# Other byte offsets for the operands of the split-fp32 matmuls in a four-layer encoder trunk

## Chip, cores and metric

One core of a Trainium2 chip runs the whole program. The metric is the time of one execution on the device, in microseconds (us).

## What is computed

The reference is a trunk of four layers for 256 tokens of width 1024: RWKV-7 time mixing in layers 0 and 3, stick-breaking attention in layer 1, sparse attention over selected keys in layer 2. Each layer is followed by a SwiGLU block of inner width 2816, and every sub-layer has an RMS norm ahead and a residual add behind:

```
for i in range(DEPTH):
    h = rms_norm(x, norm_mix[i])
    ...
    x = x + y
    x = x + swiglu(rms_norm(x, norm_ffn[i]), ffn_w_gu[i], ffn_w_down[i])

def swiglu(h, w_gu, w_down):
    g, u = jnp.split(h @ w_gu, 2, axis=-1)
    return (jax.nn.silu(g) * u) @ w_down
```

All of it is in float32.

## The kernel before, in words

Activations lie transposed: 128 features on the partitions, 256 tokens along them. Weights come from memory in pieces of 128 x 1024 float32 values (512 KB), each by one DMA on the queue of SyncE into one of four tiles `raw`.

Most products are made not as plain fp32 matmuls but of three fp32r matmuls. `piece` (line 905) rounds a weight piece to `wh` (a copy to fp32r on ScalarE or VectorE) and takes the rest `wl = raw - wh` (VectorE, line 913). Activations are split in the same way, into a high half and a low half that lie behind each other. Then `x*w` is `xh*wh + xl*wh + xh*wl`. The weight tiles are the stationary operand, loaded into the array by LDWEIGHTS, 128 columns (512 bytes of a partition) at a time, and the activations are the moving operand, read as a stream of 256 or 512 columns. There are five slots of 4096 bytes in a partition for `wh` and four for `wl`, counted out by the planner; one of the tiles `wh0` to `wh3` and `wl0` to `wl4` names each of them.

Three shapes of such products matter here.

- A *pair* (`gemm1`, line 955, and the down projection in `ffn`): a stream of 512 columns, `xh` and `xl` behind each other, against `wh`, then one of 256 columns, `xh`, against `wl`. The tiles `gate`, `up`, `dn` and `qk` are made of pairs. While the stream of 512 runs, the following `wl` is loaded; while that of 256 runs, the next `wh`.
- A *triple* (`mm3`, in `gemm2`, line 966, and `out_half`, line 979): three streams of 256 columns, against `wh`, `wh` again and `wl`. These are `kp`, `rp` and `po`, and `pg`.
- A *turned* triple (`v_gemm`, line 1626, and its like): the weights are the moving operand, 512 columns of `wh`, `wl` and `wh`, and the activations `xg` are loaded. These are `vps`, `k`, `q` and `qi`.

The moving activations lie in four large slots of 16 KB: `xb` (`xg`, for pairs and turned triples), `SA`, `SZ` and `PR` (`h` of the SwiGLU blocks; `prx` of `rp` is in `SZ`, `kx` of `kp` in `PR`). The activations of `po` (`yhl`, `ohl`) lie in two other slots, `s0` and `s1`.

The order of all instructions is planned beforehand: `Plan.schedule` simulates the engines with a table of costs, and `Plan.emit` writes the instructions out in that order. The costs take no account of where a tile lies. `emit` first allocates the tiles of SBUF in the order of the list `LAYOUT` (line 65), one behind the other, each rounded up to 32 bytes. A name such as `SA_0` is a slot. So a tile's address follows from what stands ahead of it in `LAYOUT`. In the version before, the constant `eps_rms` (4 bytes, hence 32) stands ahead of `xb_0 SZ_0 PR_0 SA_0`.

In the addresses of the built program that gives these remainders by 128 bytes:

| tiles | before |
|---|---|
| `wh`, `wl`, `raw` | 0, 0, 0 |
| `xb`, `SZ`, `PR`, `SA` | 32 |
| `s0`, `s1` (`yhl`, `ohl`) | 0 |
| `s6`, `s7` (`gus` and others), `xt` | 0 |

Of the kernel before, what the change touches and what calls it, by code (L numbers as in the profile page):

```python
# [14 lines left out]
F32R = mybir.dt.float32r  # L15
# [18 lines left out]
PIECE = 1024  # L34
# [22 lines left out]
for _n, _w in CONSTS:  # L57
# [6 lines left out]

LAYOUT = (
    "ones xt0 chmask xt1 xt2 xt3 sqa_0 QC_0 sq_0 s0_0 raw_0 s1_0 t_0 s6_0 raw_1 raw_2 t_1 t_2 t_3 raw_3 wh_0 wl_0 "
    "wh_1 wh_2 wh_3 t2_0 xm_0 t2_1 xm_1 xm_2 consts0 wl_1 xm_3 identb t2_2 wl_2 t_4 t2_3 wl_3 s7_0 t2_4 dc_0 vf0 vf1 "
    "vf3 vf2 t_5 t_6 t_7 kc0_0 kc1_0 kc2_0 eps_rms xb_0 SZ_0 PR_0 SA_0 lim eps_gn vecs omka kks_0").split()


class Region:
# [759 lines left out]
def trunk(ctx: ExitStack, tc: tile.TileContext, xT_in, vecs_in, wts, lora_in, consts_in, id32_in, nqk_in, outT, order, layers=None):  # L831
# [11 lines left out]
    def T(shape, group=None, name="t", dtype=F32):  # L843
        return plan.tile(sb, [P] + list(shape), dtype, group, name)
# [41 lines left out]
    identb = T([P], name="identb", dtype=BF16)  # L886
    eps_rms, eps_gn = T([1], name="eps_rms"), T([1], name="eps_gn")
    anye.memset(eps_rms, 1e-6)
    lim = T([2], name="lim")
# [3 lines left out]
    omka = T([2, NC], name="omka")  # L893
# [7 lines left out]
    def f(ap):  # L901
        return ap.bitcast(F32)


    def piece(key):

        i = len(order)
        order.append(key)
        r = T([PIECE], "raw", f"raw{i}")
        sp.dma_start(r, wts[i])  # L910
        h, l = T([PIECE], "wh", f"wh{i}", F32R), T([PIECE], "wl", f"wl{i}", F32R)
        anye.copy(h, r)
        dve.tensor_tensor(l, r, f(h), op=ALU.subtract)
        return h, l
# [40 lines left out]
    def gemm1(key, x, name, group="g"):  # L955


        out = bank(name, group)
        wh, wl = [v3(t, NC) for t in piece(key)]
        for c in range(NC):  # L960
            with unit():
                pe.matmul(out, wh[:, c], flat(x[:, c]), start=(c == 0), stop=False)
                pe.matmul(out[:, :S], wl[:, c], x[:, c, 0], start=False, stop=(c == NC - 1))
        return out

    def gemm2(key, xs, name):

        out = bank(name, "g")
        for c in range(NC):
            if c % 4 == 0:  # L970
                wh, wl = [v3(t, 4) for t in piece(key + (c // 4,))]
            with unit():
                for i in range(2):
                    sl = slice(i * P, (i + 1) * P)
                    mm3(out[:, i * S:(i + 1) * S], (wh[:, c % 4, sl], wl[:, c % 4, sl]), xs(c),
                        start=(c == 0 and i == 0), stop=(c == NC - 1 and i == 1))
        return out

    def out_half(key, half, xs, after):

        for j in range(4):
            o = bank("po", "g")
            wh, wl = [v3(t, 4) for t in piece(key + (half, j))]
            for k in range(4):
                with unit():
                    for n in range(2):
                        sl = slice(n * P, (n + 1) * P)
                        mm3(o[:, n * S:(n + 1) * S], (wh[:, k, sl], wl[:, k, sl]), xs(k),
                            start=(k == 0 and n == 0), stop=(k == 3 and n == 1))
            dve.tensor_tensor(xt[j], xt[j], ab(o), op=ALU.add)  # L990
            if half == 1:
                after(j)
# [1108 lines left out]
```

## Time and profile before

| | |
|---|---|
| median of 3 runs | 1358.36 us (1357.81 to 1359.17) |
| the profiled execution | 1358.13 us |
| its span in the profile | 1356.1 us |
| TensorE clock granted, mean | 0.999 |
| instructions | 26070 |

A profile is one execution, taken by the hardware profiler. PE is TensorE's matmuls and PEld its weight loads, DVE is VectorE, ACT ScalarE, POOL GpSimd and SP SyncE, whose queue issues the DMAs. Nearly every instruction carries line 827, where `emit` writes it out, so groups are told apart by the names of their tiles. The recorded duration of a matmul reaches from its start to an end that is modelled, and the next one starts before that: the spacing of the starts is what TensorE takes. Some records of matmuls can be missing.

### The profile page before, as it was taken

What the parts mean: (1) busy time and instruction counts of PE and PEld (TensorE: products, weight loads), DVE (VectorE), ACT (ScalarE), POOL (GpSimd) and SP (SyncE); (2) the same over time, 40 slices, a digit from 0 to 9 for tenths busy, and PEclk for the clock granted to TensorE, in tenths of its full rate; (3) what the DMA queues carried; (4) which work ended last, traced back from release to release, by engine and by line L of the source; (5) the groups of instructions that cost most, each with busy time, mean ns of one, the idle gap of its engine ahead of it and who ended that gap; (6) DMA issues with size and microseconds to landing.
All of it is one profiled execution on the core that took longest, in us unless ns stands there. A gap on an engine that the chain in (4) does not pass through costs nothing.

```text
span 1356.1 us, 26070 instructions
## 1 busy us (share of the span) xinstructions
PE 1335.6 (98%) x10480; PEld 1168.0 (86%) x10480; DVE 1119.4 (83%) x1932; ACT 777.9 (57%) x1301; POOL 8.8 (1%) x22
## 2 busy tenths in 40 slices
PE   8999899999999999999999999999999999999998
PEld 7997798888888898888887798888899877988887
DVE  8998789886676779886679988888589997988864
ACT  7945665545466755544456876555378366655442
POOL 0000000000000000000000000000000000000000
PEclk9999999999999999999999999999999999999999
DMA  6423255555655345556664545656544232556653
GB/s 247 145 85 122 65 171 187 189 191 178 209 171 156 123 147 188 185 192 202 196 185 139 175 129 186 187 188 192 195 127 131 74 111 81 171 186 188 188 187 121
DMA packets 61336, 220.09 MB, mean 162 GB/s; under 512 B 6816, under 2 KB 8352, under 8 KB 60960
## 3 DMA queue, kind: packets, MB, share of 16 engines
q1 hardware_dynamic: 61216, 218.44, 50.5%
q8 instruction: 82, 1.34, 0.4%
q14 instruction: 38, 0.31, 0.1%
HBM read 217.36 MB, written 1.05 MB: 161 GB/s over the span
## 4 chain that ended last, share of the span: by engine, by line
PE 90%; DVE 7%; issue 1%; DMA 1%; ACT 1%; SPq 0%; DVEq 0%; ACTq 0%
PE gate L827 18%; PE up L827 18%; PE dn L827 17%; PE po L827 7%; PE vps L827 3%; PE qk L827 3%; PE kp L827 3%; PE rp L827 3%; PE z L827 2%; PE vp L827 2%; PE q L827 2%; PE k L827 2%; PE chain L827 1%; DVE inv L827 1%; PE attn_o L827 1%
## 5 line engine op out<-in xcount | busy, mean ns | idle before, releaser
L827 ACT CAST wh<-raw 128x1024 fp32r<-128x1024 f32 x351 | 367.1, 1051 | 342.5 <-PE dn L827 96.4
L827 DVE TENSOR_TENSOR wl<-raw,wh 128x1024 fp32r<-128x1024 f32 x383 | 461.4, 1220 | 85.4 <-ACT wh L827 64.4
L827 PE MATMUL gate<-xg,wh 128*128 128x512 f32 x704 | 263.2, 392 | 0.0
L827 PE MATMUL up<-xg,wh 128*128 128x512 f32 x704 | 263.0, 393 | 0.0
L827 PE MATMUL dn<-h,wh 128*128 128x512 f32 (+1 forms) x720 | 244.5, 387 | 0.0
L827 PE MATMUL gate<-xg,wl 128*128 128x256 f32 x704 | 196.8, 280 | 0.0
L827 PE MATMUL dn<-h,wl 128*128 128x256 f32 x704 | 196.8, 279 | 0.0
L827 PE MATMUL up<-xg,wl 128*128 128x256 f32 x704 | 196.8, 279 | 0.0
L827 PEld LDWEIGHTS dn<-h,wh 128*128 128x128 f32 x720 | 134.0, 188 | 28.7
L827 PEld LDWEIGHTS up<-xg,wh 128*128 128x128 f32 x704 | 132.1, 188 | 29.1
L827 PEld LDWEIGHTS gate<-xg,wh 128*128 128x128 f32 x704 | 132.1, 188 | 29.0
L827 PEld LDWEIGHTS gate<-xg,wl 128*128 128x128 f32 x704 | 132.2, 188 | 0.1
L827 PEld LDWEIGHTS up<-xg,wl 128*128 128x128 f32 x704 | 132.1, 188 | 0.1
L827 PEld LDWEIGHTS dn<-h,wl 128*128 128x128 f32 x704 | 132.2, 188 | 0.0
L827 PE MATMUL vp<-xv,raw 128*128 128x256 f32 x256 | 57.4, 382 | 0.6 <-PE qct L827 0.6
L827 DVE TENSOR_TENSOR gus<-gus,rstd 128x512 f32<-128x512 f32 x88 | 56.9, 681 | 0.1
L827 ACT CAST h<-gus 128x512 fp32r<-128x512 f32 x42 | 26.1, 621 | 53.4 <-DVE gus L827 53.1
L827 PEld LDWEIGHTS vp<-xv,raw 128*128 128x128 f32 x256 | 47.8, 190 | 8.1 <-PE qct L827 0.8
L827 DVE TENSOR_TENSOR h<-gus,h 128x512 fp32r<-128x512 f32 x44 | 30.4, 690 | 25.5 <-ACT h L827 25.5
L827 PE MATMUL rp<-prx,wh 128*128 128x256 f32 x256 | 50.4, 297 | 0.0
L827 PE MATMUL kp<-kx,wh 128*128 128x256 f32 x256 | 47.6, 286 | 0.9 <-DVE kx L827 0.8
L827 PE MATMUL po<-yhl,wh 128*128 128x256 f32 x256 | 48.2, 290 | 0.0
(327 smaller groups left out, 2354.7 us busy)
## 6 DMA issues: line engine op xcount, KB each, us to landing
raw<-in_wts_dram SPq DMA_DIRECT2D x401, 512.0 KB, 3.8
lora<-in_lora_dram SPq DMA_DIRECT2D x2, 1280.0 KB, 10.1
xt<-in_xT_dram SPq DMA_DIRECT2D x4, 256.0 KB, 4.0
lora<-in_lora_dram SPq DMA_DIRECT2D x2, 512.0 KB, 6.0
inv<-in_id_dram SPq DMA_DIRECT2D x2, 512.0 KB, 3.5
out_dram<-xt SPq DMA_DIRECT2D x8, 128.0 KB, 1.9
sbt<-in_consts_dram SPq DMA_DIRECT2D x1, 512.0 KB, 3.5
consts<-in_consts_dram SPq DMA_DIRECT2D x1, 288.0 KB, 9.2
```

The source lines that it names most:

```text
L827: getattr(getattr(nc, o.eng), method)(*map(real, args), **{k: real(a) for k, a in kw.items()})
```

## The change

The two large edits are in the places of tiles. In `LAYOUT`, `PR_0`, `xb_0`, `SZ_0` and `SA_0` go to places ahead of `eps_rms`. In `piece`, the tiles of `wh` and `wl` get 32 more columns (128 bytes), and the 1024 columns that are used begin 16 columns (64 bytes) into `wh` and 4 columns (16 bytes) into `wl`.

```
 LAYOUT = (
     "ones xt0 chmask xt1 xt2 xt3 sqa_0 QC_0 sq_0 s0_0 raw_0 s1_0 t_0 s6_0 raw_1 raw_2 t_1 t_2 t_3 raw_3 wh_0 wl_0 "
-    "wh_1 wh_2 wh_3 t2_0 xm_0 t2_1 xm_1 xm_2 consts0 wl_1 xm_3 identb t2_2 wl_2 t_4 t2_3 wl_3 s7_0 t2_4 dc_0 vf0 vf1 "
-    "vf3 vf2 t_5 t_6 t_7 kc0_0 kc1_0 kc2_0 eps_rms xb_0 SZ_0 PR_0 SA_0 lim eps_gn vecs omka kks_0").split()
+    "wh_1 wh_2 wh_3 t2_0 xm_0 t2_1 xm_1 PR_0 xm_2 consts0 wl_1 xm_3 identb t2_2 wl_2 t_4 t2_3 wl_3 s7_0 xb_0 SZ_0 "
+    "t2_4 dc_0 vf0 vf1 vf3 vf2 t_5 t_6 t_7 kc0_0 kc1_0 kc2_0 SA_0 eps_rms lim eps_gn vecs omka kks_0").split()
...
-        h, l = T([PIECE], "wh", f"wh{i}", F32R), T([PIECE], "wl", f"wl{i}", F32R)
+        h, l = (T([PIECE + 32], g, f"{g}{i}", F32R)[:, at:at + PIECE] for g, at in (("wh", 16), ("wl", 4)))
```

The remainders by 128 bytes in the built program are then:

| tiles | before | after |
|---|---|---|
| rounded weights in `wh` | 0 | 64 |
| rest in `wl` | 0 | 16 |
| `xb`, `SZ`, `PR`, `SA` | 32 | 0 |
| `s0`, `s1`, `s6`, `s7`, `xt`, `raw` | 0 | 0 |

The instructions of every engine, their order, their sizes, the semaphores that they wait for and those that they raise are the same in both programs; only addresses differ. `raw`, `s0`, `s1` and all that stands ahead of `wh_0` in `LAYOUT` stay where they were. Three other tiles in `wh` and `wl` slots, made by other lines (`wy` and `XT`), keep remainder 0.

## The prediction

> **What bounds the kernel now.** I read the profile's page first: the busy shares, then the chain that ended last.
>
> ```profile
> PE 1335.6 (98%) x10480; PEld 1168.0 (86%) x10480; DVE 1119.4 (83%) x1932; ACT 777.9 (57%) x1301; POOL 8.8 (1%) x22
> PE 90%; DVE 7%; issue 1%; DMA 1%; ACT 1%; SPq 0%; DVEq 0%; ACTq 0%
> PE gate L827 18%; PE up L827 18%; PE dn L827 17%; PE po L827 7%; PE vps L827 3%; PE qk L827 3%; PE kp L827 3%; PE rp L827 3%; PE z L827 2%; PE vp L827 2%; PE q L827 2%; PE k L827 2%; PE chain L827 1%; DVE inv L827 1%; PE attn_o L827 1%
> ```
>
> The chain is matmuls for 90% of the span, and the split products (gate, up, dn, po, vps, qk, kp, rp, q, k) make up most of it. Whatever changes the spacing of those matmuls changes the time nearly one for one. VectorE is next with 83%, so I read it stage by stage: here a stretch of gate and up, then one of dn.
>
> ```profile
> 255.00:305.00 50.00, 50.00 (x290) 44.00 (x289) 44.44 (x69) 24.66 (x31) 0.00 (x0) 1.00 0.61 193
> 305.00:365.00 60.00, 60.00 (x348) 52.84 (x347) 39.17 (x52) 28.94 (x34) 0.00 (x0) 1.00 0.59 190
> ```
>
> After the length of the stretch stand PE, PEld, DVE and ACT with their busy times. PE has no gap in either, the granted clock is 1.00, and VectorE is busy for 44.44 of 50 us, 89%, in the first, 65% in the second.
>
> The spacing is read from the timeline of a few pairs.
>
> ```profile
> 270.06 0.39 PE L827 MATMUL gate<-xg,wh 128*128 128x512 f32 x1
> 270.06 0.19 PEld L827 LDWEIGHTS gate<-xg,wl 128*128 128x128 f32 x1
> 270.29 0.28 PE L827 MATMUL gate<-xg,wl 128*128 128x256 f32 x1
> 270.29 0.19 PEld L827 LDWEIGHTS up<-xg,wh 128*128 128x128 f32 x1
> 270.40 0.39 PE L827 MATMUL up<-xg,wh 128*128 128x512 f32 x1
> ...
> 272.14 0.39 PE L827 MATMUL gate<-xg,wh 128*128 128x512 f32 x1
> ```
>
> Six pairs take 272.14 - 270.06 = 2.08 us, 346.7 ns each; within one, the stream of 512 columns takes 0.23 us and that of 256 about 0.12. Each weight load starts together with a stream: so two reads of the same partition run side by side, and how their addresses stand to each other could matter. That is all that this change touches.
>
> Next, the groups of matmuls, shapes apart. The last number of a row is the idle time before the group: nearly none.
>
> ```profile
> L827 PE MATMUL gate<-xg,wh 128*128 128x512 f32 x704 | 263.2, 392 | 0.0
> L827 PE MATMUL up<-xg,wh 128*128 128x512 f32 x704 | 263.0, 393 | 0.0
> L827 PE MATMUL gate<-xg,wl 128*128 128x256 f32 x704 | 196.8, 280 | 0.0
> L827 PE MATMUL dn<-h,wl 128*128 128x256 f32 x704 | 196.8, 279 | 0.0
> L827 PE MATMUL qk<-xg,wl 128*128 128x256 f32 x128 | 35.8, 279 | 0.0
> L827 PE MATMUL po<-yhl,wl 128*128 128x256 f32 x128 | 36.1, 282 | 0.0
> L827 PE MATMUL po<-ohl,wl 128*128 128x256 f32 x128 | 36.1, 282 | 0.0
> L827 PE MATMUL rp<-prx,wl 128*128 128x256 f32 x128 | 35.9, 281 | 0.0
> L827 PE MATMUL kp<-kx,wl 128*128 128x256 f32 x128 | 35.9, 281 | 0.0
> L827 PE MATMUL k<-wl,xg 128*128 128x512 f32 x32 | 12.6, 392 | 0.0
> L827 PE MATMUL k<-wh,xg 128*128 128x512 f32 x64 | 20.8, 396 | 0.0
> L827 PE MATMUL vps<-wl,xg 128*128 128x512 f32 x64 | 25.2, 394 | 0.0
> ```
>
> A duration is longer than the spacing by a constant: a pair records 392 + 280 = 672 ns and takes 346.7, so each record is about 163 ns over. Differences of durations within one shape are therefore differences of spacing.
>
> For the least that a stream costs I take the warm-up matmuls, bf16 and 256 columns wide (in this view: smallest, median and largest duration).
>
> ```profile
> L1935 PE MATMUL warm_o<-warm_x x66: 272/273/422, 1.2 to 1141.3; 128*128 128x256 bf16 x66
> ```
>
> 273 against 280: an fp32r stream of 256 columns is 7 ns over the bf16 one, some 6% of its 117 to 119 ns of spacing. Something slows it. If it grows with the width, a stream of 512 is some 14 ns over (an estimate, twice 7).
>
> **The change part by part.** No instruction is added, removed or moved, and no wait; the tables of remainders say what is new. The streams that count are these. Pairs: 704 each of gate, up and dn and 128 of qk, 2240 in all, at 346.7 ns: 776.6 us. Triples: kp, rp and two of po, each 128 `wl` streams with twice as many `wh` streams, 4 x 384 = 1536 streams at about 119 ns (282 - 163): 183 us. Turned triples (vps, k, q, qi) are some 430 streams of about 231 ns (394 - 163): 100 us. Together 1060 of 1356 us, so 1% of spacing is 10.6 us, 0.8% of the time.
>
> *What remainders do, as far as the trace has them.* Call d the weights' remainder less the stream's. In kp, rp and the pairs d is -32 (96 of 128); in po it is 0; in turned triples the roles are swapped, loads at 32 and streams at 0, so d is +32. In triples the step from d = 0 to -32 is one from 282 to 281 ns: 1 ns. For 512 columns, d = -32 (gate) has 392 and d = +32 (k: 64 at 396 and 32 at 392, mean 394.7) has 2.7 ns more. So remainders have effects, of 1 to 3 ns a stream, though the groups differ in more than d. After the change d is 64 while a `wh` is loaded (beside the 256 stream of a pair) and 16 while a `wl` is loaded (beside the 512). Neither is in the trace. Bounds: the excess over bf16 may go, 7 + 14 = 21 ns a pair and 7 a triple's stream, and 14 a turned one: 2240 x 21 + 1536 x 7 + 430 x 14 = 47.0 + 10.8 + 6.0 = 63.8 us less. Or a step as from d = -32 to +32 may come on every 512, 2.7 ns, and as from the pair's 280 to po's 282 on every 256, 2 ns.
>
> I take the size of the steps seen, on the side of a gain: 2 ns at a pair's 256 stream, whose loads move from 32 to 64 bytes away, the farthest on a circle of 128 bytes; 1 ns at its 512, where d = 16 lies between two remainders that the trace has; and 1 ns at a triple's streams, which leave d = 0 (po, the slowest seen) or -32. 2240 x 3 = 6.7 us, 1536 x 1 = 1.5 us, nothing for turned triples: 8.2 us.
>
> A page puts the whole excess in another way, and nothing of the sum rests on it: the Trainium skill, "TensorE: Matmul & The Clock Gate", section "Back-to-back issue gap", gives N/2.4 + 2.5 ns for a stream of N columns once the clock is up, 215.8 ns for 512 and 109.2 for 256. By it a pair would be 325 ns, an estimate, and all of the difference to 346.7, 2240 x 21.7 = 48.6 us, would be excess; the trace's pairs do not reach it.
>
> *VectorE and ScalarE* write `wh` and `wl` at the new offsets and read `wh` back beside `raw` at 0.
>
> ```profile
> L827 DVE TENSOR_TENSOR wl<-raw,wh 128x1024 fp32r<-128x1024 f32 x383 | 461.4, 1220 | 85.4 <-ACT wh L827 64.4 <-PE dn L827 14.7 <-PE gate L827 0.3
> L827 ACT CAST wh<-raw 128x1024 fp32r<-128x1024 f32 x351 | 367.1, 1051 | 342.5 <-PE dn L827 96.4 <-issue 91.5 <-PE up L827 65.2
> L827 DVE CAST wh<-raw 128x1024 fp32r<-128x1024 f32 x32 | 22.0, 687 | 11.8 <-PE dn L827 9.5 <-PE vps L827 1.0 <-PE pg L827 0.5
> L827 DVE TENSOR_TENSOR h<-gus,h 128x512 fp32r<-128x512 f32 x44 | 30.4, 690 | 25.5 <-ACT h L827 25.5
> L827 DVE TENSOR_TENSOR gus<-gus 128x512 f32<-128x512 f32 x44 | 30.1, 684 | 0.4
> ```
>
> `h` was written and read at remainder 32 with `gus` at 0, for 690 ns; `gus` alone, all at 0, takes 684. So mixed remainders cost VectorE at most 6 ns in 684. I take nothing, and the cover is large: a piece feeds eight pairs, 2774 ns, and with 89% busy VectorE has 305 ns left per piece of gate and up. If the subtraction took over 25% longer (305 of 1220), VectorE would pace those stages. If all 32 casts fell from 687 to the subtraction's 1220 ns, that would be 17 us of VectorE time spread over the run, beside a busy PE.
>
> *DMAs* write `raw`, which stays. Wider tiles cost space alone.
>
> The sum against the profiled execution: 1358.13 - 8.2 = 1349.9, say 1350 us. That execution is 0.23 us under the median of three, so no correction is made. After a gain of 3 ns a pair VectorE would be at 90% in gate and up and still hidden.
>
> **The rivals.**
>
> *Slower: aligned streams of 512 behave like the turned ones.* In turned triples the streams start at a multiple of 128 and the loads do not, which is what all pairs become. If that is what costs 394.7 against 392, and a 256 stream at 0 costs po's 282 against 280, a pair is 2.7 + 2 = 4.7 ns longer: 2240 x 4.7 = 10.5 us, and kp and rp go from 281 to 282, 768 x 1 = 0.8 us: 1369 us. It decides when a 512 record of gate is 394 or more. For it: every row with a stream at remainder 0 is among the slower of its shape. Against it: the k row against `wl` also streams from 0 and has 392.
>
> *The same: addresses do not matter.* The rows differ by 1 to 3 ns between groups that also differ in what follows a stream (256 after 256, 512 after 512), which could be all of it; then only tiles move: 1358 us. The Trainium skill, "SBUF — State Buffer", section "Who interferes with whom", says that TensorE has independent read ports for the stream and for LDWEIGHTS and that PE and ACT never wait on anyone; by that rule the time stays. The trace neither bears it out nor refutes it: the 7 ns over bf16 show that something slows fp32r streams, not what.
>
> *Much faster.* The excess is a meeting of stream and load that the new remainders avoid for the most part. Half of the bound, 31.9 us: 1326 us. For it: an excess of 7 ns is there in every split product, at d of -32, 0 and +32, none of which is free of it. Against it: an excess so alike at three remainders looks like a property of the stream itself.
>
> That the change does not do what it says cannot be for the addresses, which the built program gives; that they do nothing is the case above.
>
> **How the numbers follow.** The forecast, a small gain, has 0.39; much faster 0.10; the same 0.21; slower 0.30. Two runs of this kernel can be told apart at about 0.2%, 2.7 us. So faster is 0.49, same 0.21, slower 0.30. The range must reach the slower rival, 1369, and go down past the forecast to near much faster; I put it from 1329 to 1369, which leaves out about half of the much faster case and those slower cases that exceed the 4.7 ns a pair, under 2 in 10 together. Of the gain's own range, from 1 ns to 8 ns a pair (2.2 to 17.9 us): 1340 to 1356.
>
> **What would show it.** The durations of gate, up and dn are the test, with their counts unchanged: the forecast has the 256 streams at 278 and the 512 streams at 391; the slower rival 282 and 394.7; the same case 280 and 392; much faster 276 and 385 or less. The po and kp rows against `wl` should both be 281 or less. On the chain, dn:
>
> ```profile
> 308.01 60.69 PE dn L827 x354
> ```
>
> should shrink by 177 x 3 ns, half a microsecond. `wl<-raw,wh` should stay at 1220 ns and the cast at 1051; VectorE's idle time before `wl` should not rise. The forecast's reasoning is wrong if matmul durations stay and the time moves, or if only one of the two stream widths moves while the other goes the other way.

## The result and the profile after

| | before | after |
|---|---|---|
| median of 6 runs each | 1358.09 us (1357.12 to 1364.42) | 1347.16 us (1346.09 to 1352.29) |
| ratio to before, 95% interval | 1 | 0.9919 [0.9895, 0.9943] |
| the profiled execution | 1358.13 us | 1346.9 us |
| its span | 1356.1 us | 1345.0 us |

The changed kernel is faster by 0.8%, and its slowest run (1352.29 us) lies below the fastest of the kernel before (1357.12 us). The two spans differ by 11.1 us. First the page of the changed kernel: its span, the busy time of each engine, and the shares of the chain that ended last, by engine and by line.

```profile
span 1345.0 us, 26070 instructions
PE 1324.5 (98%) x10480; PEld 1159.3 (86%) x10480; DVE 1116.6 (83%) x1932; ACT 776.6 (58%) x1301; POOL 9.1 (1%) x22
PE 83%; DVE 12%; ACT 3%; issue 1%; DMA 1%; SPq 0%; DVEq 0%; ACTq 0%
PE dn L827 18%; PE gate L827 18%; PE up L827 18%; PE po L827 6%; PE qk L827 3%; PE vps L827 3%; PE kp L827 3%; PE z L827 2%; DVE inv L827 2%; PE q L827 2%; PE k L827 2%; DVE xtmp L827 1%; DVE SB L827 1%; PE rp L827 1%; DVE wl L827 1%
```

PE's busy time fell by 1335.6 - 1324.5 = 11.1 us, all of the difference. What of the span PE stood idle is the same: 1356.1 - 1335.6 = 20.5 us and 1345.0 - 1324.5 = 20.5 us. So no wait came or went; the matmuls themselves became shorter. VectorE has 12% of the chain where it had 7%, but PE's idle time did not grow by that, and a still faster kernel below (1342.39 us) has 7% again. So I read it as a choice between paths that end at nearly the same time, and no new bound.

The groups of matmuls of the changed kernel, shapes apart (busy us, mean ns of one, idle time before):

```profile
L827 PE MATMUL gate<-xg,wh 128*128 128x512 f32 x704 | 260.5, 390 | 0.0
L827 PE MATMUL up<-xg,wh 128*128 128x512 f32 x704 | 260.2, 390 | 0.0
L827 PE MATMUL dn<-h,wh 128*128 128x512 f32 x688 | 238.9, 393 | 0.0
L827 PE MATMUL dn<-h,wl 128*128 128x256 f32 x704 | 196.1, 278 | 0.0
...
L827 PE MATMUL gate<-xg,wl 128*128 128x256 f32 x704 | 194.5, 276 | 0.0
...
L827 PE MATMUL kp<-kx,wl 128*128 128x256 f32 x128 | 36.0, 281 | 0.0
L827 PE MATMUL po<-ohl,wl 128*128 128x256 f32 x128 | 35.9, 281 | 0.0
L827 PE MATMUL rp<-prx,wl 128*128 128x256 f32 x128 | 35.9, 281 | 0.0
L827 PE MATMUL po<-yhl,wl 128*128 128x256 f32 x128 | 35.9, 280 | 0.0
L827 PE MATMUL qk<-xg,wl 128*128 128x256 f32 x128 | 35.5, 277 | 0.0
```

Gate and up gained on both streams: 392 and 393 became 390, 280 and 279 became 276. `dn` did not. Its 512 stream had before

```profile
L827 PE MATMUL dn<-h,wh 128*128 128x512 f32 x688 | 239.0, 392 | 0.0
```

and went to 393; its 256 stream went from 279 to 278. `po` went from 282 to 281 and 280, `kp` and `rp` stayed at 281, `qk` went from 279 to 277.

The timeline of the changed kernel, in a stretch of gate and up (start in us, duration):

```profile
269.40 0.39 PE L827 MATMUL gate<-xg,wh 128*128 128x512 f32 x1
269.63 0.28 PE L827 MATMUL gate<-xg,wl 128*128 128x256 f32 x1
269.75 0.39 PE L827 MATMUL up<-xg,wh 128*128 128x512 f32 x1
...
271.44 0.39 PE L827 MATMUL gate<-xg,wh 128*128 128x512 f32 x1
```

Six pairs take 271.44 - 269.40 = 2.04 us, 340 ns each, where six took 2.08 us before.

In `dn` the same timeline shows pairs of both kinds:

```profile
338.62 0.39 PE L827 MATMUL dn<-h,wh 128*128 128x512 f32 x1
...
338.95 0.39 PE L827 MATMUL dn<-h,wh 128*128 128x512 f32 x1
...
339.30 0.40 PE L827 MATMUL dn<-h,wh 128*128 128x512 f32 x1
...
339.65 0.40 PE L827 MATMUL dn<-h,wh 128*128 128x512 f32 x1
...
340.00 0.39 PE L827 MATMUL dn<-h,wh 128*128 128x512 f32 x1
```

In whole nanoseconds of the trace the first two pairs take 340 ns each, the next two 353 and 350. At 339.30 the stream moves from a slot `SA` to `SZ`; the four large slots no longer stand alike. By 256 bytes, `xb` and `SZ` are at 0 and `SA` and `PR` at 128; before, all four were at the same remainder. Of the 38 runs of short pairs in `dn`, 37 end where the stream changes between `SA` or `PR` and `SZ`, and none at a change from `PR` to `SA`.

To compare kernels I take the mean spacing of the pairs from the starts in each trace. Before: gate and up 346.7 ns, `dn` 346.7; no pair is under 342 ns, and the spacings repeat after six pairs, with 230 ns at every second stream of 512 and 228 or 229 at the others (512 and 256 columns by turns: 230, 117, 228, 118, 230, 117, 228, 119, 230, 116, 229, 118 ns). After: gate and up 340.5, with 95% of the pairs under 342 and a rhythm that repeats after one pair (226 to 227, then 113 to 114); `dn` 346.5, with 39% under 342 and most of the others at 229 to 238 and 115 to 122 ns.

The short rhythm is not there from the first pair. In the changed kernel's four stages of gate and up it sets in after 0, 3, 23 and 17 slower pairs, and then lasts but for a few breaks. In `dn` each step between the two kinds of slots puts the pairs out of it, and pairs after a step stay slow for a while even where the stream stays in one slot.

The gain is then: gate and up 1408 x 6.2 = 8.7 us; `dn` 704 x 0.2 = 0.1; `qk`, from 346.7 to 342.6, 128 x 4.1 = 0.5; `po`, from about 119.0 to 117.9 ns a stream, 768 x 1.1 = 0.8; `kp` and `rp` 768 x 0.3, about 0.3; turned triples, from 233.4 to 231.9 ns a stream, 430 x 1.5 = 0.6. Together 11.0 of the 11.1 us. (Spacings with another instruction between are left out of these means.)

The other engines in the changed kernel, first its stretches of gate and up and of `dn` (length, PE, PEld, DVE, ACT), then the rows of the subtraction and the cast:

```profile
255.00:305.00 50.00, 50.00 (x295) 44.23 (x294) 44.73 (x70) 25.96 (x33) 0.00 (x0) 1.00 0.58 189
305.00:365.00 60.00, 60.00 (x350) 52.64 (x349) 38.19 (x51) 28.36 (x34) 0.00 (x0) 1.00 0.60 194
```

```profile
L827 DVE TENSOR_TENSOR wl<-raw,wh 128x1024 fp32r<-128x1024 f32 x383 | 461.1, 1220 | 83.5 <-ACT wh L827 67.1 <-PE dn L827 10.2
```

```profile
L827 ACT CAST wh<-raw 128x1024 fp32r<-128x1024 f32 x351 | 365.9, 1049 | 332.4 <-PE dn L827 93.7 <-issue 89.2 <-PE up L827 59.1
```

VectorE is at 44.73 of 50 us, PE still has no gap there, and both durations are those of before (1220 and 1051).

### The profile page after: what moved, and what is told of

Read it like the earlier page. It is cut to its first block, busy times and chain, and to the rows that moved or that the text cites. A ratio compares the mean times of both kernels' runs of the same rounds, so it can differ in the third digit from the quotient of the medians.

```text
span 1345.0 us, 26070 instructions
## 1 busy us (share of the span) xinstructions
PE 1324.5 (98%) x10480; PEld 1159.3 (86%) x10480; DVE 1116.6 (83%) x1932; ACT 776.6 (58%) x1301; POOL 9.1 (1%) x22
## 4 chain that ended last, share of the span: by engine, by line
PE 83%; DVE 12%; ACT 3%; issue 1%; DMA 1%; SPq 0%; DVEq 0%; ACTq 0%
PE dn L827 18%; PE gate L827 18%; PE up L827 18%; PE po L827 6%; PE qk L827 3%; PE vps L827 3%; PE kp L827 3%; PE z L827 2%; DVE inv L827 2%; PE q L827 2%; PE k L827 2%; DVE xtmp L827 1%; DVE SB L827 1%; PE rp L827 1%; DVE wl L827 1%
## 5 line engine op out<-in xcount | busy, mean ns | idle before, releaser
L827 ACT CAST wh<-raw 128x1024 fp32r<-128x1024 f32 x351 | 365.9, 1049 | 332.4 <-PE dn L827 93.7
L827 DVE TENSOR_TENSOR wl<-raw,wh 128x1024 fp32r<-128x1024 f32 x383 | 461.1, 1220 | 83.5 <-ACT wh L827 67.1
L827 PE MATMUL gate<-xg,wh 128*128 128x512 f32 x704 | 260.5, 390 | 0.0
L827 PE MATMUL up<-xg,wh 128*128 128x512 f32 x704 | 260.2, 390 | 0.0
```

The lines of the kernel that those rows point to most:

```text
L827: getattr(getattr(nc, o.eng), method)(*map(real, args), **{k: real(a) for k, a in kw.items()})
```

## The experiments

Throughout, d is the load's remainder by 128 bytes less the stream's, first for `wh` (loaded beside a stream of 256), then for `wl` (beside one of 512). Before has (-32, -32), after (64, 16). Every ratio is to the kernel before, run on the same chip, with the 95% interval. "LAYOUT of before" means that the list of slots is put back, so that the streams are at 32 and the four large slots are alike by 256. The tiles with 32 more columns make the slots of `wh` and `wl` 4224 bytes long instead of 4096; this too is part of the change. The built programs have four slots for each of the two (not five for `wh`). By 256 bytes all eight start at 0 before; with 4224 bytes those of `wh` start at 0, 0, 128 and 0, those of `wl` at 128, 128, 0 and 128.

**The first four: one side alone, or differences?** Theory 1: the difference of loads and stream counts, wherever both stand. Against it: one side does it alone, the streams at multiples of 128 bytes or the offsets of the weights.

*Streams alone moved* (d = 0, 0):

```diff
-for g, at in (("wh", 16), ("wl", 4)))
+for g, at in (("wh", 0), ("wl", 0)))
```

> Only the streams' slots move to remainder 0; the rounded weights and their rest go back to 0, so the difference d (load less stream) is 0 everywhere. Theory 1, the difference is what counts: the gain is gone, since d = 0 was po's and the slowest seen (282 ns for 256 columns): gate's two streams at 392 and 280 ns or more, 1358 to 1366 us. Theory 2, aligned streams are what helps: gate at 390 and 276 to 278 ns, 1347 to 1352 us.

Measured: 1363.14 us, 1.0033 [1.002, 1.0046], slower than before. Its rows of gate:

```profile
L827 PE MATMUL gate<-xg,wh 128*128 128x512 f32 x704 | 264.8, 395 | 0.0
...
L827 PE MATMUL gate<-xg,wl 128*128 128x256 f32 x704 | 197.8, 281 | 0.0
```

395 and 281 against 392 and 280: aligned streams alone, with the longer slots, bring a loss, so they are not what the change gains by.

*Weights alone moved* (d = 32, -16): LAYOUT of before, offsets 16 and 4 kept.

> Only the weights' offsets of 64 and 16 bytes; the streams stay at 32, so d is 32 for wh and -16 for wl in the pairs, and 64 and 16 in po alone. Theory 1 (the difference): po as in the changed kernel (280 to 281 ns against wl), the pairs lose most of their gain: between 1352 and 1366 us. Theory 2b, the weights' own offset is what helps: gate at 390 and 276 ns, 1347 to 1350 us.

Measured: 1361.37 us, 1.0028 [1.0018, 1.0038]; gate 393 and 280. The offsets alone bring nothing either. Each half of the change loses, and both together gain.

*Differences of before at the places of after* (d = -32, -32): LAYOUT of after, and

```diff
-for g, at in (("wh", 16), ("wl", 4)))
+for g, at in (("wh", 24), ("wl", 24)))
```

> Streams at 0, both weights at 96: all addresses are new, but d is -32 in the pairs, as in the kernel before. Theory 1 (the difference by 128 bytes): gate at 392 and 280 ns, 1356 to 1360 us. Theory 2 (aligned streams): 1347 to 1352 us.

Measured: 1364.6 us, 1.0048 [1.003, 1.0066]. This missed what theory 1 expected, which was the time of before: its pairs take 350.4 ns in gate and up, not 346.7. By 128 bytes all differences are those of before, so something else counts too; it has steps of 128 of 256 bytes, between slots of weights and between slots of streams, and before has none.

*Differences of after at the places of before* (d = 64, 16): LAYOUT of before, and

```diff
-for g, at in (("wh", 16), ("wl", 4)))
+for g, at in (("wh", 24), ("wl", 12)))
```

> Streams at 32, rounded weights at 96 and rest at 48: no operand at the remainders of the changed kernel, but d is 64 and 16 in the pairs. Theory 1 (the difference): gate at 390 and 276 ns, dn as scattered as in the changed kernel, 1345 to 1350 us. Theory 2 (aligned streams): gate at 392 and 280 ns, 1356 us or more.

Measured: 1342.39 us, 0.9881 [0.9867, 0.9896]; the span is 1339.2 us. Its groups:

```profile
L827 PE MATMUL gate<-xg,wh 128*128 128x512 f32 x704 | 260.5, 390 | 0.0
...
L827 PE MATMUL dn<-h,wh 128*128 128x512 f32 x688 | 234.5, 389 | 0.0
...
L827 PE MATMUL dn<-h,wl 128*128 128x256 f32 x704 | 194.4, 276 | 0.0
```

Its chain has for a run of `dn` where the changed kernel has 60.88 us:

```profile
304.14 59.55 PE dn L827 x354
```

Gate is as in the changed kernel, with streams at 32 instead of 0, which bears theory 1 out for the gain. And here `dn` gains as well, which theory 1 had not expected (it had `dn` scattered and 1345 us at least). It has 389 and 276: 340.1 ns a pair, 99% of them under 342, against 346.5 and 39% in the changed kernel. That is 704 x 6.4 = 4.5 us, most of the 5.8 us between the two spans. What this kernel has and the changed one has not is streams alike by 256 bytes.

**Three on steps of 256 bytes.** Theory A: a step of 128 of 256 bytes between one stream and the next breaks the short rhythm, and that is why `dn` gained nothing. Against it: the exact place of the streams (0 or 32), or where the weights stand.

*Streams alike by 256, at remainder 0* (d = 64, 16): offsets 16 and 4 of the change, and in the LAYOUT of before

```diff
-    ... kc2_0 eps_rms xb_0 SZ_0 PR_0 SA_0 lim eps_gn vecs omka kks_0
+    ... kc2_0 xb_0 SZ_0 PR_0 SA_0 eps_rms lim eps_gn vecs omka kks_0
```

> The changed kernel (streams at 0, weights at 64 and 16) with the four slots of the streams behind each other, so that all four have the same remainder by 256 bytes; in the changed kernel SA and PR are 128 bytes off SZ and xb by 256. Theory A, a change of the streams' remainder by 256 breaks the short rhythm of the pairs: dn pairs at 340 ns like gate and up, 1340 to 1344 us. Theory B, the absolute places of the runs before (32, 96, 48) are better than 0, 64, 16: dn scattered as in the changed kernel, 346 to 347 ns a pair, 1346 to 1349 us.

Measured: 1343.38 us, 0.9875 [0.9847, 0.9903], the span 1340.4. `dn`:

```profile
L827 PE MATMUL dn<-h,wh 128*128 128x512 f32 x688 | 234.5, 389 | 0.0
...
L827 PE MATMUL dn<-h,wl 128*128 128x256 f32 x704 | 194.4, 276 | 0.0
```

The differences and remainders by 128 are those of the change; only the slots are alike by 256, and `dn` is at 340.1 ns a pair.

*Streams apart by 256* (d = 64, 16): the kernel of 1342.39 us with a small tile moved between `SZ` and `PR`.

```diff
-    ... s7_0 t2_4 dc_0 vf0 ... eps_rms xb_0 SZ_0 PR_0 SA_0 ...
+    ... s7_0 t2_4 vf0 ... eps_rms xb_0 SZ_0 dc_0 PR_0 SA_0 ...
```

> The kernel with 32, 96 and 48 and one 128-byte tile moved between the slots SZ and PR, so that xb and SZ differ from PR and SA by 128 of 256 bytes; remainders by 128 stay. Theory A: the dn pairs lose their rhythm wherever the slot of the stream changes between those two groups, 344 to 348 ns a pair, 1345 to 1349 us. Theory B: dn stays at 340 ns, 1340 to 1344 us.

Measured: 1346.74 us, 0.9898 [0.9875, 0.9922], the span 1344.9.

```profile
L827 PE MATMUL gate<-xg,wh 128*128 128x512 f32 x704 | 260.3, 390 | 0.0
...
L827 PE MATMUL dn<-h,wh 128*128 128x512 f32 x688 | 238.9, 393 | 0.0
...
L827 PE MATMUL dn<-h,wl 128*128 128x256 f32 x704 | 196.1, 279 | 0.0
```

Gate and up, whose streams lie all in `xb`, keep the gain; `dn`, which steps between slots, loses it: 346.5 ns and 39% under 342, the very numbers of the changed kernel. Theory A holds in both directions. It is the step that counts and not the place by 256: `xb` is at 0, 32, 128 and 160 by 256 in the four kernels with (64, 16), and gate has 390 in each.

`qk`, whose streams also lie all in `xb`, is not explained by this: its pairs take 346.6 and 344.5 ns in the two kernels that are alike by 256, and 342.6 and 342.3 in the two that are not, with 51% and 62% of them short against 75% and 81%. Why is not shown; it is 128 pairs, half a microsecond.

*All 96 bytes on* (d = -32, -32): the kernel before with its tiles of 4096 bytes; the small constants moved ahead of `wh_0` push weights and large slots by the same amount.

```diff
-    ... raw_3 wh_0 ... wl_3 s7_0 ... kc2_0 eps_rms xb_0 SZ_0 PR_0 SA_0 lim eps_gn vecs omka kks_0
+    ... raw_3 eps_rms lim eps_gn wh_0 ... wl_3 kks_0 s7_0 ... kc2_0 xb_0 SZ_0 PR_0 SA_0 vecs omka
```

> The kernel before with 96 bytes put ahead of the weights and 32 behind them: weights at 96, streams at 0, difference -32 as before, slots of 4096 bytes, so that all weights have one remainder by 256. The third run had the same remainders by 128 with slots of 4224 bytes, and was slower than the kernel before. Theory 1 with A (differences, and steady remainders by 256): pairs of 346.7 ns, 1356 to 1360 us. Theory 2 (the absolute remainders 0 and 96 are worse): pairs of 349 to 351 ns, 1362 to 1367 us.

Measured: 1358.57 us, 0.9992 [0.9978, 1.0005].

```profile
L827 PE MATMUL gate<-xg,wh 128*128 128x512 f32 x704 | 263.2, 392 | 0.0
...
L827 PE MATMUL gate<-xg,wl 128*128 128x256 f32 x704 | 196.7, 279 | 0.0
```

Pairs are at 346.7 ns in gate, up and `dn`, as before. The streams are at multiples of 128 and the weights at 96, as in the kernel of 1364.6 us, and the time is that of before. So a move of both sides together does nothing. What is left, of all that was looked at here, to make that other kernel lose in gate and up, whose streams all lie in `xb`, is the unlike places of its weights' slots by 256. No run changed that alone, but the trace of that kernel points the same way. With its addresses matched to it in order, the 1037 pairs of gate and up whose `wl` stands, against the stream, 128 bytes off its place of before by 256 take 351.0 ns, and the 348 where it stands as before take 348.5. After's differences do not mind: gate and up have 340.1 to 340.6 ns in all four combinations of slots.

**Five on the differences.** All have the LAYOUT of before, streams alike by 256, and wider tiles; only the two offsets change. They ask whether each stream has a price of its own by its d, as the prediction had it, or the two belong together.

*`wh` at 64, `wl` at no distance* (64, 0):

```diff
+for g, at in (("wh", 24), ("wl", 8)))
```

> Streams at 32 as in the fourth run, rounded weights at 96 (d = 64), rest at 32 (d = 0): the offset of the rounded weights alone. If the load of wh beside the 256 stream is what gains: pairs of 342 to 344 ns, 1345 to 1350 us. If it needs the offset of wl: pairs of 347 to 350 ns, 1358 to 1365 us.

Measured: 1355.44 us, 0.9971 [0.9953, 0.9989]; gate 392 and 277, 346.1 ns a pair, between the two expectations. 45% of the pairs of gate and up and 52% of those of `dn` are short; the others are slow. Addresses matched to the trace show which. Where `wl` is at no distance by 256 too, the pairs of gate and up take 344.4 ns and 60% are short; where it is 128 bytes off by 256 (348 of the pairs), they take 351.3 ns and none is short. So here, unlike with (64, 16), the remainder by 256 decides.

*`wl` at 16 alone* (0, 16), *both at 64* (64, 64), *swapped* (16, 64):

```diff
+for g, at in (("wh", 8), ("wl", 12)))
...
+for g, at in (("wh", 24), ("wl", 24)))
...
+for g, at in (("wh", 12), ("wl", 24)))
```

> Streams at 32, rounded weights at 32 (d = 0), rest at 48 (d = 16): the offset of the rest alone, the four slots alike by 256. If the load of wl beside the 512 stream is what gains: pairs of 340 to 344 ns, 1342 to 1349 us. If both offsets are needed: the short rhythm is rare, pairs of 346 ns or more, 1355 to 1364 us.

> Streams at 32, both weights at 96 (d = 64 for both): is 16 bytes for the rest needed, or is the farthest place good for both loads, as the prediction supposed of wh? If 64 is good for every load: pairs of 340 ns, 1340 to 1345 us. If the rest needs its own place: pairs of 344 ns or more, 1350 to 1362 us.

> Streams at 32, rounded weights at 48 (d = 16), rest at 96 (d = 64): the two offsets swapped. If the pairing of each load with its stream matters: no short rhythm, pairs of 347 to 351 ns, 1358 to 1366 us. If any two unlike places do: pairs of 340 ns, 1340 to 1345 us.

Measured: 1364.7 us, 1.0037 [1.002, 1.0054]; 1364.89 us, 1.0039 [1.0023, 1.0055]; 1364.11 us, 1.0034 [1.0021, 1.0047]. The pairs take 350.3, 349.9 and 349.6 ns; the first two kernels are a little slower than any expectation had them. Gate with both at 64:

```profile
L827 PE MATMUL gate<-xg,wh 128*128 128x512 f32 x704 | 264.7, 394 | 0.0
...
L827 PE MATMUL gate<-xg,wl 128*128 128x256 f32 x704 | 197.2, 280 | 0.0
```

Beside the 256 stream `wh` is as far off as in the change, and yet that stream records 280 and not 276. How long it takes depends on the other load as well.

*The rest 16 bytes below instead of above* (64, -16):

```diff
+for g, at in (("wh", 24), ("wl", 4)))
```

> Streams at 32, rounded weights at 96 (d = 64), rest at 16 (d = -16). If only the distance of the rest's load counts, as the prediction's circle has it: pairs of 340 ns, 1340 to 1345 us. If the sign counts: pairs of 344 ns or more, 1350 to 1362 us.

Measured: 1360.08 us, 1.0015 [0.9999, 1.003]; 348.0 ns, with 11% short. Sixteen bytes to the other side don't do it: the sign counts, and the distance alone is not enough.

All spacings of gate and up, from the starts in the traces:

| d of `wh`, `wl` | bytes of a weights' slot | ns a pair | under 342 ns | us |
|---|---|---|---|---|
| 64, 16 (after; streams apart) | 4224 | 340.5 | 95% | 1347.16 |
| 64, 16 (streams at 32, alike) | 4224 | 340.6 | 95% | 1342.39 |
| 64, 16 (streams at 0, alike) | 4224 | 340.7 | 94% | 1343.38 |
| 64, 16 (streams at 32, apart) | 4224 | 340.2 | 98% | 1346.74 |
| 64, 0 | 4224 | 346.1 | 45% | 1355.44 |
| -32, -32 (before) | 4096 | 346.7 | 0% | 1358.09 |
| -32, -32 (all 96 on) | 4096 | 346.7 | 0% | 1358.57 |
| 64, -16 | 4224 | 348.0 | 11% | 1360.08 |
| 32, -16 | 4224 | 348.4 | 0% | 1361.37 |
| 0, 0 (streams apart) | 4224 | 349.3 | 4% | 1363.14 |
| 16, 64 | 4224 | 349.6 | 2% | 1364.11 |
| 64, 64 | 4224 | 349.9 | 0% | 1364.89 |
| 0, 16 | 4224 | 350.3 | 0% | 1364.7 |
| -32, -32 (places of after) | 4224 | 350.4 | 0% | 1364.6 |

The last column has runs on several chips, on which the kernel before had medians between 1357.72 and 1359.67 us; rows that differ by less than 2 us are better compared by their pairs.

Two of these kernels beat both the one before and the one after: 1342.39 and 1343.38 us. They keep the differences of the change and hold the four stream slots alike by 256 bytes.

## Why the prediction was right, and where it was not

**What bounds the kernel: right.** The spacing of the matmuls set the time one for one: 11.1 us less busy PE, 11.1 us less span, and PE idle for the same 20.5 us.

**The sum: right in sign, 8.2 us forecast and 11.1 measured, but by other terms.** The step that failed is the price list, "2 ns at a pair's 256 stream, whose loads move from 32 to 64 bytes away, the farthest on a circle of 128 bytes; 1 ns at its 512". It gave 3 ns to each of 2240 pairs. Gate and up gained 6.2 ns, qk 4.1, `dn` 0.2: 8.7 + 0.5 + 0.1 = 9.3 us for the 6.7 forecast. Too small a price on most pairs was partly paid back by a third of them that got nothing. That the sum came so near is luck. The sign was luck too: it was a choice ("on the side of a gain"), as neither new difference was in the trace, and of the other differences that were tried only (64, 0) gained at all.

**The reason behind the prices: wrong.** Distance on a circle of 128 bytes is not what counts. Both loads at 64 gave 349.9 ns; 64 and 16 swapped gave 349.6; 16 to the other side gave 348.0. And a stream has no price of its own by its d: the 256 stream at d = 64 records 276 with `wl` at 16, 277 on the mean with `wl` at 0, and 280 with `wl` at 64. What the differences 64 and 16 do together is to let the pairs fall into a rhythm of 340 ns that repeats after every pair.

**The part on `dn`: wrong, by the test it gave itself.** The prediction would be wrong in its reasoning if one stream width went the other way; in `dn` the 512 went from 392 to 393 and the 256 from 279 to 278 (by the spacing of the starts, 229.2 to 230.6 and 117.5 to 115.9 ns). The chain's piece of `dn` did not shrink by half a microsecond; it takes, in the changed kernel,

```profile
304.62 60.88 PE dn L827 x354
```

for 60.69. The prediction's tables hold remainders by 128 bytes only, and by those all four stream slots are alike in both kernels. By 256 bytes the new LAYOUT sets `SA` and `PR` apart from `xb` and `SZ`, and the kernels with and without that step show its price: 346.5 and 340.1 ns a pair, and 1346.74 against 1343.38 us on one chip.

**Triples: right in size for `po`, too much for the others.** 1536 streams at 1 ns were to give 1.5 us; `po` gave about 1.1 ns and 0.8 us, `kp` and `rp` 0.3 ns and 0.3 us. All records against `wl` are at 281 or less, as forecast. Turned triples gave 0.6 us, where nothing was put down.

**VectorE and ScalarE: right.** 1220 and 1049 ns after, against 1220 and 1051, and 1220 to 1222 and 1049 to 1051 in all the experiments, with offsets of 0, 16, 32, 48, 64 and 96 bytes. VectorE's idle time before `wl` fell from 85.4 to 83.5 us.

**The rivals.** *The same* is refuted: nothing but addresses differs between these kernels, and they reach from 1342.39 to 1364.89 us. The rule of the Trainium skill, "SBUF — State Buffer", section "Who interferes with whom", by which PE never waits on anyone and has independent read ports for the stream and for LDWEIGHTS, does not carry as far as the prediction took it, that the time stays: how the addresses of weights and stream stand to each other moved a pair from 340 to 350 ns. That the two reads meet somewhere is a likely reason, but no view of the profile shows it. *Slower by aligned streams* is refuted for this change, gate having 390 where the rival needed 394 or more; but aligned streams with weights left at 0 do lose, 1363.14 us, and the 4.7 ns a pair that it asked is near what several differences cost: 350 against 346.7. *Much faster* is refuted as well: 390, not 385, though the 256 streams of gate and up did reach the 276 that it asked. The best pairs measured, 340.1 ns, are still 15 ns over the 325 that the prediction estimated from the formula in the Trainium skill, "TensorE: Matmul & The Clock Gate", section "Back-to-back issue gap", which the section calls the gap of an isolated matmul.

**What stays open.** Why 64 and 16 allow the short rhythm throughout, (64, 0) in part, and no other pair that was tried for more than 11% of the pairs, is not shown; no view of the profile shows reads of SBUF. Every run with other differences than those of before had weights' slots of 4224 bytes, unlike by 256. With before's differences such a kernel takes 3.7 ns a pair more, and with (64, 0) the remainder by 256 of the `wl` slot parts short pairs from slow ones. Whether (64, 0), (64, 64) or (0, 0) would do better with these slots alike by 256 was not tried, and why the short rhythm needs up to 23 pairs to set in is not shown. Nor was it tried whether another d lets triples and turned triples gain.

## What to carry to other kernels

Where back-to-back fp32r matmuls bound a kernel, the places of the weights and the activations in a partition are worth a trial of their own: read the spacing of the starts from the timeline before and after, since here a change of 0.8% came without any wait appearing or going. Move both sides by the same amount as a control (it should do nothing), then one side against the other, and try combinations, since the effects of the two loads did not add up separately here. Try them with all tiles that follow one another in the same role alike by 256 bytes, and look at remainders by more than the one step that the change speaks of.

## What the runs showed of the hardware that was not expected

- A pair of fp32r matmuls (512 and 256 columns) takes 340.1 to 350.6 ns on the mean by nothing but its addresses. In the kernel before the spacings repeat every six pairs; in the changed kernel's gate and up every pair, once that rhythm has set in, after 0 to 23 pairs.
- By 128 bytes the relation of weights and streams is what counts: both moved on together by 96 bytes left all at 346.7 ns and 1358.57 us, and the differences 64 and 16 gave 340 ns with streams at 0 and at 32.
- A step of 128 of 256 bytes from one stream to the next ends the short rhythm: in two kernels of different LAYOUT that have this step `dn` came to the same 346.5 ns with the same 39% of short pairs, and in two without it to 340.1 with 99%.
